# Input and block-boundary norms of a two-block network: from one token tile at a time to two

## The chip, the cores and the metric

The kernel runs on one core of one Trainium2 chip. The metric is the device time of one execution in microseconds (us); lower is better. Engines are named as in the profile: PE is TensorE, PEld its weight loads, DVE is VectorE, ACT is ScalarE, POOL is GpSimd, SP is SyncE (here it only issues DMAs). The result is one float32 tensor of 512 x 1024.

## The reference, cut to what matters

Two networks of two layers each run one after the other on 512 tokens of width 1024. The first begins with a layer norm of the input, and each of its layers ends in another; the second begins each half layer with an RMS norm that is scaled and shifted by a modulation vector:

```python
x = layer_norm(x, ln0_g, ln0_b)
for l in range(2):
    mix = hybrid_mixer(x, w_in[l], ...)
    x = layer_norm(alpha * x + mix, ln1_g[l], ln1_b[l])
    hid = square(relu(x @ w_up[l]))
    x = layer_norm(alpha * x + hid @ w_down[l], ln2_g[l], ln2_b[l])
for l in range(2):
    h = rms_norm(x, g_mix[l]) * (1.0 + sc_m) + sh_m
    z = h @ w_in_2[l] + b_in[l]
    ...
```

So the last layer norm of the first network (l = 1) is followed at once by the first RMS norm of the second. This place is called the boundary below; the norm of the input is called the start.

## The kernel before, in words

**Tiles.** The 512 tokens lie in four token tiles of 128 (tk = 0 to 3), 128 tokens on the partitions and 1024 features along the free axis. A matmul needs its activations the other way round, features on the partitions: `xTh` and `xTl`, the high and low part of a float32 number in two float32r tiles of 128 x 8 x 512. Every product is three matmuls (L235 to L237: high by high, then the two mixed ones). Weights come as 512 KB chunks (`wraw`, three buffers, issued on SP, L224), are rounded on ACT (`whi`, L228), and the rest is subtracted on DVE (`wlo`, L229).

**A norm of one tile.** `layer_norm` (L347) takes the statistics of two halves (`bn_stats`, L345), joins them (`bn_aggr`, L351), forms the reciprocal square root of the variance in `rsqrt` (L306) and applies both in one DVE instruction over the tile (L354). `rsqrt` has no table: it is an integer start value and three Newton steps on DVE. On a 128 x 1 operand that is nine instructions, three to start (L311, L316, L317) and three times two (L323, L324), each of which reads what the one before it wrote. On any other shape a step takes three (L326 to L328), twelve in all. `affine_T` (L356) then turns the tile: eight PE transposes (L336) in two halves into PSUM tiles `tr` (two buffers), eight ACT instructions that apply gain and offset column by column (`hT`, L364, operands `lnc` or `ge`, `mc`), and for each half a cast to `xTh` (DVE, L365) and a subtraction to `xTl` (L366; first half on DVE, second half on POOL). `lag` holds back `affine_T` in program order for one or two tiles.

**The start.** `first` (L1215) issues on SP the small table `cpack` (identity), the four tiles of `x`, the large table (L194), the two gain and offset columns `lnc` (L373), then the per-layer vectors and the first weight chunks. `norm_out` (L1016) takes the tiles one after another; the statistics of tiles 1 to 3 are ordered on DVE behind the norm of tile 0 (`issue_after`). The first product is the one for q: `lin_fm` with `early=2` (L256) makes two output tiles in two cuts of 256 tokens, so its first matmuls need token tiles 0 and 1, and its second cut tiles 2 and 3. `bias_setup` (L398) loads a one-hot table and the bias table on SP and prepares them with three DVE instructions (L407, L408, L411) for small matmuls that run much later (L416).

**The boundary.** The last product of the first network adds up in PSUM for the four token tiles in turn; `ffn1` (L963) adds each to `xo` (L989) and calls `after` (L1182). For the last layer that is, tile by tile: statistics, `bn_aggr` (L1190), subtract the mean and multiply by the gain row (L1192), `rsqrt`, multiply and add the offset row (L1195), a DMA out, the sum of squares on ACT (`Square` with an accumulator, L1199, into one of the two buffers `xhat`), and then `rms_tile` (L1307): a second `rsqrt`, a scaled copy on ACT into the same `xhat` (L1326), and `affine_T`. `rms_tile` of a tile is called one tile later than its layer norm, tiles 2 and 3 both at the end. Next in PE's order are the first gate tiles of the second network, again `early=2` in two cuts.

**What sets the order.** A planner orders the instructions of each engine when the program is built: of those whose inputs it believes ready it takes the earliest in program order. So the small instructions of one `rsqrt` are laid between the long ones of other tiles. On the chip each engine then runs its list in order.

Of the kernel before, what the change touches and what calls it, by code (L numbers as in the profile page):

```python
# [10 lines left out]
F32 = mybir.dt.float32  # L11
# [9 lines left out]
D = 1024  # L21
# [146 lines left out]
class Kern:  # L168
# [18 lines left out]
    def load_constants(self):  # L187
# [14 lines left out]
        nc.vector.memset(self.halfpi, math.pi / 2)  # L202

# [143 lines left out]
    def layer_norm(self, r, st):  # L347

        nc = self.nc
        mv = self.sm.tile([128, 2], F32, name="bnmv")  # L350
        nc.vector.bn_aggr(out=mv, in_=st)  # L351
        rs = self.sm.tile([128, 1], F32, name="rstd")
        self.rsqrt(rs, mv[:, 1:2], 1.0, self.e_ln)
        return nc.vector.tensor_scalar(r, r, mv[:, 0:1], rs, op0=OP.subtract, op1=OP.mult)  # L354
# [641 lines left out]
    def norm_tile(self, wk, pp, r, st, cols, tk, act, xd, lag):  # L996

        last = self.layer_norm(r, st)

        def turn():  # L1000
            self.affine_T(wk, pp, r, tk, cols[:, 0, :], cols[:, 1, :], act)
            self.nc.gpsimd.dma_start(xd[:, tk, :], r)

        self.lag(tk, turn, lag)
        return last
# [10 lines left out]
    def norm_out(self, wk, pp, r, cols, xd, act):  # L1016
        st = self.new_stats(wk)
        first = None
        for tk in range(4):
            with self.tc.issue_after(first.ins) if tk else ExitStack():  # L1020
                for half in range(2):
                    self.stats(st[:, tk], r[:, tk, :], half)
            done = self.norm_tile(wk, pp, r[:, tk, :], st[:, tk], cols, tk, act, xd, FILL["lag"][0])
            first = first or done

    def layer1(self, l, xd, act, start):
# [3 lines left out]
        with tc.tile_pool(name="mx", bufs=1) as mx:  # L1030
# [6 lines left out]
            with tc.tile_pool(name="at", bufs=2) as wk:  # L1037
# [31 lines left out]
                if l == 0:  # L1069
                    self.bias_setup(wk, pp)  # L1070
                    self.zero_images(wk)
# [102 lines left out]
        with tc.tile_pool(name="f1", bufs=1) as wk:  # L1174
# [6 lines left out]

            def after(tk, ch):  # L1182
# [5 lines left out]
                if last:  # L1188
                    mv = self.sm.tile([128, 2], F32, name="bnmv")
                    nc.vector.bn_aggr(out=mv, in_=st[:, tk])  # L1190
                    x = xo[:, tk, :]
                    nc.vector.scalar_tensor_tensor(out=x, in0=x, scalar=mv[:, 0:1], in1=g2, op0=OP.subtract, op1=OP.mult)  # L1192
                    rs = self.sm.tile([128, 1], F32, name="rstd")
                    self.rsqrt(rs, mv[:, 1:2], 1.0, self.e_ln)
                    nc.vector.scalar_tensor_tensor(out=x, in0=x, scalar=rs, in1=b2, op0=OP.mult, op1=OP.add)  # L1195
                    nc.gpsimd.dma_start(xd2[:, tk, :], x)
                    ss = self.sm.tile([128, 1], F32, name="rss")
                    xn = wk.tile([128, D], F32, name="xhat", bufs=2)
                    nc.scalar.activation(xn, x, AF.Square, accum_out=ss)  # L1199
                    box.append((x, ss, xn))  # L1200
                    for t in ((), (0,), (1,), (2, 3))[tk]:
                        xt, sst, xnt = box[1 + t]
                        self.rms_tile(wk, pp, xt, t, 0, 0, box[0], ss=sst, xn=xnt, lag=FILL["lag"][3])
# [11 lines left out]
    def first(self):  # L1215
# [6 lines left out]
        def start(wk):  # L1222
            xin = wk.tile([128, 4, D], F32, name="xin")
            for tk in range(4):
                nc.sync.dma_start(xin[:, tk, :], a["x"][tk * 128:(tk + 1) * 128, :])
            self.load_constants1()
            cols = self.ln_cols(wk, (0, 1))
# [79 lines left out]
    def rms_tile(self, wk, pp, x, tk, l, i, act, st=None, bufs=3, ss=None, xn=None, lag=0):  # L1307
# [3 lines left out]
        rs = self.sm.tile([128, 1], F32, name="rstd")  # L1311
        if ss is not None:
            self.rsqrt(rs, ss, 1.0 / D, self.e_rms)
        else:
# [494 lines left out]
```

## Time and profile before

| | us |
|---|---|
| median of 3 runs | 3738.05 (3736.97 to 3739.5) |
| the profiled execution | 3742.39 |
| its span, first instruction to last | 3740.6 |
| PE busy in the span | 3598.2 (96%) |
| DVE busy | 2237.3 (60%) |
| ACT busy | 1408.4 (38%) |
| POOL busy | 121.9 (3%) |

The profiled execution took 3742.39 us and its span covers 3740.6 of them; it lies 4.34 us above the median of the runs. Times in the rows further down are counted from the span's start. A busy share of PE holds waiting inside a pipelined matmul too, so where PE lost time is read from the stretches in which it had nothing to do, and from the clock it was granted there.

### The profile page before, as it was taken

To read this page: it belongs to the slowest core of one execution; us is meant where nothing else is said; L and a number is where in the kernel's file an instruction comes from. 1 tells how busy PE (TensorE), PEld (TensorE's weight loads), DVE (VectorE), ACT (ScalarE), POOL (GpSimd) and SP (SyncE) were. 2 spreads that over 40 slices of the span, in tenths; PEclk is the share of its full clock that TensorE was granted. 3 is DMA by queue.
4 is the path that set the end of the run, shared out by engine and by line. 5 is a ranking of instruction groups with operands and counts; after the bars stand their busy time and mean duration, and the time that the engine had idled before them with its cause. 6 is when DMAs were issued, how large, how long until landed. Compare 5 with 4: busy or idle time off the path is not lost. (4 is left out here: it accounts for less than half of the span.)

```text
span 3740.6 us, 54252 instructions
## 1 busy us (share of the span) xinstructions
PE 3598.2 (96%) x21232; PEld 2844.9 (76%) x21232; DVE 2237.3 (60%) x4799; ACT 1408.4 (38%) x2413; POOL 121.9 (3%) x209
## 2 busy tenths in 40 slices
PE   7999999899999999998999999999999999999999
PEld 6677776778877877766788777778888877778887
DVE  5667775765566577756745549765333479664333
ACT  4543333332334543332424234554222344633221
POOL 0000000000000000000000000000000000000000
PEclk9999999999999999999999999999999999999999
DMA  4333333555543333234655432334332323253322
GB/s 147 119 114 85 88 84 121 162 182 180 167 157 91 104 93 92 78 98 151 197 178 171 156 105 71 119 122 149 96 96 97 116 86 107 67 186 119 96 96 96
DMA packets 509520, 452.23 MB, mean 121 GB/s; under 512 B 88112, under 2 KB 405232, under 8 KB 509264
## 3 DMA queue, kind: packets, MB, share of 16 engines
q1 hardware_dynamic: 492032, 400.88, 35.1%
q0 software_dynamic: 10320, 32.15, 2.5%
q10 hardware_dynamic: 6912, 15.73, 1.2%
q8 instruction: 167, 2.74, 0.3%
q14 instruction: 89, 0.73, 0.1%
HBM read 395.68 MB, written 53.01 MB: 120 GB/s over the span
## 5 line engine op out<-in xcount | busy, mean ns | idle before, releaser
L229 DVE TENSOR_TENSOR wlo<-wraw,whi 128x1024 fp32r<-128x1024 f32 (+2 forms) x496 | 604.4, 1219 | 775.1 <-ACT whi L228 769.3
L228 ACT ACTIVATE whi<-wraw 128x1024 fp32r<-128x1024 f32 (+2 forms) x496 | 523.3, 1055 | 1419.8 <-PE tm L237 563.4
L235 PE MATMUL acc<-xTh,whi 128*128 128x512 f32 (+1 forms) x2320 | 913.0, 394 | 5.7 <-ACT whi L228 2.1
L237 PE MATMUL acc<-xTh,wlo 128*128 128x512 f32 (+1 forms) x2320 | 901.6, 389 | 3.5 <-DVE wlo L229 3.5
L236 PE MATMUL acc<-xTl,whi 128*128 128x512 f32 (+1 forms) x2320 | 897.1, 387 | 3.9 <-POOL xTl L366 1.9
L235 PEld LDWEIGHTS acc<-xTh,whi 128*128 128x128 f32 x2320 | 437.1, 189 | 106.8 <-issue 14.9
L237 PEld LDWEIGHTS acc<-xTh,wlo 128*128 128x128 f32 x2320 | 437.7, 189 | 93.0 <-DVE wlo L229 5.1
L236 PEld LDWEIGHTS acc<-xTl,whi 128*128 128x128 f32 x2320 | 438.1, 189 | 84.6 <-POOL xTl L366 4.0
L235 PE MATMUL tm<-whi,hidh 128*128 128x512 f32 x784 | 307.2, 392 | 1.3 <-DVE xo L989 1.2
L237 PE MATMUL tm<-whi,hidl 128*128 128x512 f32 x784 | 306.5, 391 | 0.0
L236 PE MATMUL tm<-wlo,hidh 128*128 128x512 f32 x784 | 306.5, 391 | 0.0
L236 PE MATMUL tm<-wlo,xTh 128*128 128x512 f32 (+1 forms) x448 | 169.7, 379 | 14.1 <-DVE wlo L229 14.1
L235 PEld LDWEIGHTS tm<-whi,hidh 128*128 128x128 f32 x784 | 147.2, 188 | 35.8 <-issue 2.0
L237 PEld LDWEIGHTS tm<-whi,hidl 128*128 128x128 f32 x784 | 147.2, 188 | 32.2
L236 PEld LDWEIGHTS tm<-wlo,hidh 128*128 128x128 f32 x784 | 147.2, 188 | 31.8
L237 PE MATMUL tm<-whi,xTl 128*128 128x512 f32 (+1 forms) x448 | 168.9, 377 | 0.0
L235 PE MATMUL tm<-whi,xTh 128*128 128x512 f32 (+1 forms) x448 | 167.7, 378 | 0.0
L1293 DVE SCALAR_TENSOR_TENSOR asum<-araw,cc,asum 128x768 f32<-128x768 f32 x112 | 113.8, 1016 | 43.5 <-DMA araw<-in_w_ada_dram 42.4
L1716 DVE TENSOR_TENSOR hT<-hT,acc 128x512 f32<-128x512 f32 x44 | 30.3, 688 | 132.5 <-PE acc L237 128.8
L236 PEld LDWEIGHTS tm<-wlo,xTh 128*128 128x128 f32 x448 | 85.4, 191 | 29.6 <-DVE wlo L229 15.0
L569 DVE CUSTOM_DVE_ANT_0 L<-lg,G 128x512 f32<-128x512 f32 (+3 forms) x128 | 73.5, 587 | 47.2 <-PE lg L1507 31.2
L570 ACT ACTIVATE L<-L,ast 128x384 f32<-128x384 f32 (+3 forms) x128 | 71.1, 556 | 69.8 <-DVE ast L569 68.9
(479 smaller groups left out, 5454.7 us busy)
## 6 DMA issues: line engine op xcount, KB each, us to landing
wraw<-in_w_in_dram SPq DMA_DIRECT2D x182, 512.0 KB, 3.9
wraw<-in_w_down_dram SPq DMA_DIRECT2D x108, 512.0 KB, 3.5
araw<-in_w_ada_dram SPq DMA_DIRECT2D x128, 384.0 KB, 3.9
wraw<-in_w_gu_dram SPq DMA_DIRECT2D x88, 512.0 KB, 3.8
wraw<-in_w_up_dram SPq DMA_DIRECT2D x64, 512.0 KB, 4.2
wraw<-in_w_out_dram SPq DMA_DIRECT2D x32, 512.0 KB, 3.6
wraw<-in_w_branch_dram SPq DMA_DIRECT2D x18, 512.0 KB, 3.5
prd<-gt POOLq DMA_DIRECT2D x32, 256.0 KB, 2.7
```

Of the source, the lines that this page charges most:

```text
L228: nc.scalar.activation(hi[:, :n], raw[:, :n], AF.Copy)
L229: nc.vector.tensor_tensor(out=lo[:, :n], in0=raw[:, :n], in1=hi[:, :n].bitcast(F32), op=OP.subtract)
L235: nc.tensor.matmul(ps, st[0], mv[0], start=start, stop=False)
L236: nc.tensor.matmul(ps, st[0], mv[1], start=False, stop=False)
L237: nc.tensor.matmul(ps, st[1], mv[0], start=False, stop=stop)
L569: nc.vector.tensor_tensor_reduce(L, ps, bias, -1.0, -LOW, OP.add, OP.min, nmx)
L570: nc.scalar.activation(L, L, AF.Exp, bias=nmx, scale=-1.0, accum_out=ssum)
L1293: nc.vector.scalar_tensor_tensor(out=acc, in0=w, scalar=cc[:, k:k + 1], in1=acc, op0=OP.mult, op1=OP.add)
L1716: nc.vector.tensor_tensor(out=t[j], in0=t[j], in1=ps, op=OP.mult)
```

## The change

The norm of the input and the layer norm and RMS norm at the boundary work on pairs of token tiles: one `rsqrt` of 128 x 2 for two tiles in place of two of 128 x 1. At the start the second pair's statistics are ordered behind the norm of tile 1. At the boundary the closing instructions of tiles 0 and 1 wait for the pair's root, and both RMS norms of a pair share a root, which is called behind the opening instructions of tile 2 for the first pair and at the end for the second. The one-tile chains of the other norms stay. Further: a first small ACT instruction in `load_constants`; the `lnc` loads move from behind the large table to behind the first tile of `x`; and `bias_setup`'s DVE instructions are ordered behind the norm of tile 3.

```diff
@@ -200,6 +200,8 @@
         self.fr = g("fr", 8)
         self.halfpi = self.cst.tile([128, 1], F32, name="halfpi")
         nc.vector.memset(self.halfpi, math.pi / 2)
+        warm = self.sm.tile([128, 1], F32, name="rstd")
+        nc.scalar.activation(warm, self.halfpi, AF.Identity)
 
     def dump(self, name, ap):
         if self.dumpf:
@@ -351,7 +353,7 @@
         nc.vector.bn_aggr(out=mv, in_=st)
         rs = self.sm.tile([128, 1], F32, name="rstd")
         self.rsqrt(rs, mv[:, 1:2], 1.0, self.e_ln)
-        return nc.vector.tensor_scalar(r, r, mv[:, 0:1], rs, op0=OP.subtract, op1=OP.mult)
+        nc.vector.tensor_scalar(r, r, mv[:, 0:1], rs, op0=OP.subtract, op1=OP.mult)
 
     def affine_T(self, wk, pp, x, tk, g, b, act, bufs=3):
 
@@ -995,14 +997,15 @@
 
     def norm_tile(self, wk, pp, r, st, cols, tk, act, xd, lag):
 
-        last = self.layer_norm(r, st)
-
+        self.layer_norm(r, st)
+        self.norm_end(wk, pp, r, cols, tk, act, xd, lag)
+
+    def norm_end(self, wk, pp, r, cols, tk, act, xd, lag):
         def turn():
             self.affine_T(wk, pp, r, tk, cols[:, 0, :], cols[:, 1, :], act)
             self.nc.gpsimd.dma_start(xd[:, tk, :], r)
 
         self.lag(tk, turn, lag)
-        return last
 
     def lag(self, tk, f, lag):
 
@@ -1014,14 +1017,25 @@
         return wk.tile([128, 4, 2, 6], F32, name="bnst", bufs=1)
 
     def norm_out(self, wk, pp, r, cols, xd, act):
+
         st = self.new_stats(wk)
-        first = None
-        for tk in range(4):
-            with self.tc.issue_after(first.ins) if tk else ExitStack():
-                for half in range(2):
-                    self.stats(st[:, tk], r[:, tk, :], half)
-            done = self.norm_tile(wk, pp, r[:, tk, :], st[:, tk], cols, tk, act, xd, FILL["lag"][0])
-            first = first or done
+        for t0 in (0, 2):
+            mv, rs = self.pair()
+            with self.tc.issue_after(self.normed.ins) if t0 else ExitStack():
+                for i in range(2):
+                    for half in range(2):
+                        self.stats(st[:, t0 + i], r[:, t0 + i, :], half)
+                    self.nc.vector.bn_aggr(out=mv[:, i, :], in_=st[:, t0 + i])
+                self.rsqrt(rs, mv[:, :, 1], 1.0, self.e_ln, tag="rp")
+            for i in range(2):
+                x = r[:, t0 + i, :]
+                self.normed = self.nc.vector.tensor_scalar(x, x, mv[:, i, 0:1], rs[:, i:i + 1],
+                                                           op0=OP.subtract, op1=OP.mult)
+                self.norm_end(wk, pp, x, cols, t0 + i, act, xd, FILL["lag"][0])
+
+    def pair(self):
+
+        return (self.sm.tile([128, 2, 2], F32, name="bnmv2", bufs=2), self.sm.tile([128, 2], F32, name="rstd2", bufs=2))
 
     def layer1(self, l, xd, act, start):
         nc, a, tc, pp = self.nc, self.a, self.tc, self.pp
@@ -1067,7 +1081,8 @@
                 self.lin_tm(pp, w_in, [(1536, 2048)], act, 8,
                             lambda t, ps: nc.scalar.activation(v[:, t, :], ps, AF.Copy))
                 if l == 0:
-                    self.bias_setup(wk, pp)
+                    with tc.issue_after(self.normed.ins):
+                        self.bias_setup(wk, pp)
                     self.zero_images(wk)
                 ya = yh("ya")
                 self.pool_branch(wk, pp, l, vec, act, ya)
@@ -1179,6 +1194,16 @@
             st = self.new_stats(wk)
             box = []
 
+            late = []
+
+            def rms(t0):
+                ss, xn = late.pop()
+                rs = self.sm.tile([128, 2], F32, name="rrs2", bufs=2)
+                self.rsqrt(rs, ss, 1.0 / D, self.e_rms, tag="rp")
+                for j in range(2):
+                    self.rms_tile(wk, pp, xo[:, t0 + j, :], t0 + j, 0, 0, box[0], rs=rs[:, j:j + 1], xn=xn[j],
+                                  lag=FILL["lag"][3])
+
             def after(tk, ch):
                 self.stats(st[:, tk], xo[:, tk, :], ch)
                 if ch == 0:
@@ -1186,21 +1211,29 @@
                 if not box:
                     box.append(self.xT())
                 if last:
-                    mv = self.sm.tile([128, 2], F32, name="bnmv")
-                    nc.vector.bn_aggr(out=mv, in_=st[:, tk])
-                    x = xo[:, tk, :]
-                    nc.vector.scalar_tensor_tensor(out=x, in0=x, scalar=mv[:, 0:1], in1=g2, op0=OP.subtract, op1=OP.mult)
-                    rs = self.sm.tile([128, 1], F32, name="rstd")
-                    self.rsqrt(rs, mv[:, 1:2], 1.0, self.e_ln)
-                    nc.vector.scalar_tensor_tensor(out=x, in0=x, scalar=rs, in1=b2, op0=OP.mult, op1=OP.add)
-                    nc.gpsimd.dma_start(xd2[:, tk, :], x)
-                    ss = self.sm.tile([128, 1], F32, name="rss")
-                    xn = wk.tile([128, D], F32, name="xhat", bufs=2)
-                    nc.scalar.activation(xn, x, AF.Square, accum_out=ss)
-                    box.append((x, ss, xn))
-                    for t in ((), (0,), (1,), (2, 3))[tk]:
-                        xt, sst, xnt = box[1 + t]
-                        self.rms_tile(wk, pp, xt, t, 0, 0, box[0], ss=sst, xn=xnt, lag=FILL["lag"][3])
+                    i, x = tk % 2, xo[:, tk, :]
+                    if i == 0:
+                        box.append(self.pair())
+                    mv, rs = box[-1]
+                    nc.vector.bn_aggr(out=mv[:, i, :], in_=st[:, tk])
+                    nc.vector.scalar_tensor_tensor(out=x, in0=x, scalar=mv[:, i, 0:1], in1=g2,
+                                                   op0=OP.subtract, op1=OP.mult)
+                    if i == 0:
+                        if tk:
+                            rms(0)
+                        return
+                    self.rsqrt(rs, mv[:, :, 1], 1.0, self.e_ln, tag="rp")
+                    ss = self.sm.tile([128, 2], F32, name="rss2", bufs=2)
+                    xn = [wk.tile([128, D], F32, name="xhat", bufs=2) for _ in range(2)]
+                    for j in range(2):
+                        x = xo[:, tk - 1 + j, :]
+                        nc.vector.scalar_tensor_tensor(out=x, in0=x, scalar=rs[:, j:j + 1], in1=b2,
+                                                       op0=OP.mult, op1=OP.add)
+                        nc.gpsimd.dma_start(xd2[:, tk - 1 + j, :], x)
+                        nc.scalar.activation(xn[j], x, AF.Square, accum_out=ss[:, j:j + 1])
+                    late.append((ss, xn))
+                    if tk == 3:
+                        rms(2)
                 else:
                     self.norm_tile(wk, pp, xo[:, tk, :], st[:, tk], cols, tk, box[0], xd2, FILL["lag"][2])
 
@@ -1223,8 +1256,9 @@
             xin = wk.tile([128, 4, D], F32, name="xin")
             for tk in range(4):
                 nc.sync.dma_start(xin[:, tk, :], a["x"][tk * 128:(tk + 1) * 128, :])
+                if tk == 0:
+                    cols = self.ln_cols(wk, (0, 1))
             self.load_constants1()
-            cols = self.ln_cols(wk, (0, 1))
             self.norm_out(wk, pp, xin, cols, xd, act)
             self.dump("x0", xd)
 
@@ -1304,14 +1338,12 @@
             nc.gpsimd.dma_start(md[g * 4:g * 4 + 4, :], row[::32, :])
             yield
 
-    def rms_tile(self, wk, pp, x, tk, l, i, act, st=None, bufs=3, ss=None, xn=None, lag=0):
+    def rms_tile(self, wk, pp, x, tk, l, i, act, st=None, bufs=3, rs=None, xn=None, lag=0):
 
         nc = self.nc
         k2 = self.k2[l]
-        rs = self.sm.tile([128, 1], F32, name="rstd")
-        if ss is not None:
-            self.rsqrt(rs, ss, 1.0 / D, self.e_rms)
-        else:
+        if rs is None:
+            rs = self.sm.tile([128, 1], F32, name="rstd")
             if st is None:
                 st = self.sm.tile([128, 2, 6], F32, name="bnst")
                 for j in range(2):
```

## Rows read from the trace of the kernel before

**Rows 1.** The page, busy time, share of the span and instructions of each engine

```profile
PE 3598.2 (96%) x21232; PEld 2844.9 (76%) x21232; DVE 2237.3 (60%) x4799; ACT 1408.4 (38%) x2413; POOL 121.9 (3%) x209
```

**Rows 2.** Four stretches: us, busy time (instructions) of each engine, granted clock (PEclk), DMA share, GB/s

```profile
2147.30:2160.70 13.40, 3.97 (x17) 3.14 (x16) 13.29 (x53) 9.35 (x19) 2.92 (x4) 0.64 0.19 78
2160.70:2177.20 16.50, 15.92 (x113) 15.18 (x114) 6.04 (x17) 11.28 (x26) 5.48 (x7) 0.88 0.20 47
9.40:21.40 12.00, 5.00 (x21) 3.85 (x21) 12.00 (x45) 8.98 (x19) 2.50 (x3) 1.00 0.86 248
21.40:38.50 17.10, 14.73 (x108) 14.28 (x108) 12.61 (x26) 8.06 (x20) 4.89 (x5) 1.00 0.45 147
```

**Rows 3.** Timeline of PE at the start: start, length, what, [idle before <-releaser]

```profile
21.39 0.58 PE L235 MATMUL acc<-xTh,whi 128*128 128x256 f32 x1 [0.64 <-DVE xTh L365]
...
28.76 0.63 PE L336 MATMUL tr<-cpack,xin 128*128 128x128 f32 x4 [2.19 <-DVE xin L354]
...
38.36 0.28 PE L237 MATMUL acc<-xTh,wlo 128*128 128x256 f32 x1
```

**Rows 4.** Timeline of DVE at the start

```profile
4.80 1.29 DVE L345 BATCH_NORM_STATS2 bnst<-xin 128x6 f32<-128x512 f32 x2 [3.91 <-DMA xin<-in_x_dram]
...
6.36 0.15 DVE L311 TENSOR_SCALAR rqv<-bnmv 128x1 f32<-128x1 f32 x1
...
8.61 0.81 DVE L354 TENSOR_SCALAR xin<-xin,bnmv,rstd 128x1024 f32<-128x1024 f32 x1
...
26.03 1.75 DVE L408 TENSOR_TENSOR t<-G,t 32x512 fp32r<-32x512 f32 x1
27.81 0.81 DVE L354 TENSOR_SCALAR xin<-xin,bnmv,rstd 128x1024 f32<-128x1024 f32 x1
```

**Rows 5.** Timeline of ACT at the start

```profile
10.79 1.28 ACT L364 ACT_TABLE_LOAD   x1 [10.79 <-DMA lnc<-in_lncol_dram]
...
29.49 2.93 ACT L364 ACTIVATE hT<-tr,lnc 128x128 f32<-128x128 f32 x8 [3.67 <-PE tr L336]
```

**Rows 6.** SP's timeline at the start, and the landing times of line 1225

```profile
3.65 0.95 SPq L373 DMA_DIRECT2D lnc<-in_lncol_dram  x2
...
DMA to landing us min/median/max: 3.6/4.9/6.2
```

**Rows 7.** Line 326, the first operation of a Newton step on wider operands: ns min/median/max

```profile
L326 DVE TENSOR_TENSOR rqt<-rqy x72: 123/164/193, 156.9 to 3117.2; 128x4 f32<-128x4 f32 x30, 128x8 f32<-128x8 f32 x24, 128x32 f32<-128x32 f32 x18
```

**Rows 8.** Timeline of DVE at the boundary

```profile
2138.98 0.68 DVE L989 TENSOR_TENSOR xo<-xo,tm 128x512 f32<-128x512 f32 x1
...
2141.92 1.28 DVE L1195 SCALAR_TENSOR_TENSOR xo<-xo,rstd,lnb 128x1024 f32<-128x1024 f32 x1
2143.12 0.15 DVE L311 TENSOR_SCALAR rqv<-bnmv 128x1 f32<-128x1 f32 x1
...
2144.56 0.15 DVE L311 TENSOR_SCALAR rqv<-rss 128x1 f32<-128x1 f32 x1
...
2149.65 0.21 DVE L324 TENSOR_SCALAR rstd<-rqt,rqy 128x1 f32<-128x1 f32 x1
```

**Rows 9.** Timeline of ACT at the boundary

```profile
2149.99 1.13 ACT L1326 ACTIVATE xhat<-xo,rstd 128x1024 f32<-128x1024 f32 x1
...
2155.09 1.09 ACT L1199 ACTIVATE xhat<-xo 128x1024 f32<-128x1024 f32 x1
...
2160.94 1.16 ACT L1326 ACTIVATE xhat<-xo,rstd 128x1024 f32<-128x1024 f32 x1
...
2168.23 2.91 ACT L364 ACTIVATE hT<-tr,mc,ge 128x128 f32<-128x128 f32 x8 [0.69 <-PE tr L336]
```

**Rows 10.** Timeline of PE at the boundary

```profile
2151.17 1.97 PE L336 MATMUL tr<-cpack,xhat 128*128 128x128 f32 x8 [3.84 <-ACT xhat L1326]
...
2160.72 0.80 PE L235 MATMUL tm<-xTh,whi 128*128 128x256 f32 x2 [1.39 <-DVE xTh L365]
...
2170.99 0.38 PE L236 MATMUL tm<-xTl,whi 128*128 128x256 f32 x1 [0.22 <-DVE xTl L366]
```

## The prediction

> **What bounds the kernel now.** I read the page first: PE is busy 96% of the span [rows 1], so a norm can matter only where PE has nothing to do. The table of stretches then shows the two places that the change touches [rows 2]. At the start PE is busy 5.00 of the 12.00 us before its first product, while DVE is busy for all 12.00, and 14.73 of the 17.10 us that the first two q tiles take. At the boundary PE is busy 3.97 of 13.40 us at a granted clock of 0.64, DVE 13.29, and then 15.92 of 16.50 us at 0.88. In both, DVE sets the pace: read its timeline, then see which ACT and PE rows hang on it. Beyond them PE is full, so a shift of the first product moves the end by as much.
>
> The profiled execution took 3742.39 us, 4.34 above the median of 3738.05. The sum below is a difference within that execution, and I lay it on the median. A measurement of this kernel tells about 0.2% from no change, 7.5 us.
>
> **The start: what is removed and added.** Now tile 0's statistics start at 4.80, its root at 6.36, its norm at 8.61 [rows 4]: 1.56 us for statistics and aggregate, 2.25 for the nine-step root, 0.81 for the norm. ACT can't use it: it waits for `lnc` until 10.79 and then loads its table for 1.28 [rows 5], so `hT` of tile 0 begins at 12.07.
>
> With pairs tile 0 waits for tile 1's data. The four tiles of x land 3.6 to 6.2 us after their issues [rows 6]; with four issues at the 0.48 that SP takes for one `lnc` issue, they arrive (2.6 + 1.4)/3 = 1.3 apart, so tile 1 at 6.1. The `lnc` issues now stand ahead of it: nothing at best, their whole 0.95 at worst; I take 0.5, in the middle, as the pieces are tiny but the queue is in order. From 6.6: statistics 1.56, root 2.3, norms at 10.5 and 11.3. The root's price isn't in the trace for this shape: twelve instructions at the 0.164 of a wider one [rows 7] are 2.0, at the 0.25 per instruction of the nine-step root 3.0; I take 0.19, nearer to the first, which has the same instruction.
>
> Tile 0's transposes then start at 11.3; half of their 1.97 [rows 10] later, at 12.4, `hT` begins, now with `lnc` long landed and the table loaded. So the pair costs tile 0 only 0.3 us, and tile 1 follows without a gap: 2.93 for tile 0 [rows 5] and half of that for tile 1 give 16.8, where before its own chain held it. The first matmul, at 21.39 [rows 3], can come at 17.5 if cast and subtraction follow at once, and at 20.1 if a weight rounding on ACT (as long as another 128 x 1024 instruction there, 1.13 [rows 9]) and a weight subtraction on DVE (1.75 at worst, by the one beside a busy POOL [rows 4]) both go first. I take 19.0: **2.4 us gained**.
>
> The second gain is a stall: PE waits 2.19 us at 28.76 for the norm of tile 3 [rows 3], which starts at 27.81 right behind the bias instruction of 1.75 [rows 4]. With bias behind it and the second pair's work (two times 1.56, root 2.3, two norms 1.6: 7.0 us from 12.0, with up to 4 of other work between, since this engine is full) that norm comes at 19 to 23. I take 1.8 of the 2.19 as gained; if the planner puts those transposes early among the matmuls, all of it may stay. Together **-4.2**, between -1.3 (20.1, stall kept) and -6.1 (17.5, stall gone).
>
> At nothing: the first ACT instruction, for ACT idles until 10.79; without that cover it would cost 1.28. If the table load stayed where it is, ACT would do it while waiting for the transposes. The bias instructions move into 17.10 us in which DVE is idle 4.5; uncovered they cost 1.75 and twice 0.81 at most, ahead of the next weight subtraction. Their SP loads keep their place; the large table and tiles 1 to 3 go 0.95 later on SP, the weights not. POOL's DMAs keep their number, and it is busy 2.92 of 13.40 us at its fullest place here.
>
> **The boundary.** Tile 1's sum starts at 2138.98 [rows 8]. Its opening takes 0.68, statistics of one half and aggregate 0.9 (1.56 less 0.65), and the mean and gain instruction 1.28, by its twin of that length: 2141.85. Then the pair's root 2.3, two closing instructions 2.4 (start to start 1.20), the Square of tile 1 with its read 1.3, the second root 2.3: 2150.15 if nothing comes between. But tiles 2 and 3 open in this stretch, 5.7 us on DVE, of which 1.3 fit under that Square. That gives 2154.55; I take T = 2154.2 for the first scaled copy, because the planner fills every gap of a chain with a longer instruction, as it does between 2144.56 and 2149.65, where one root takes 5.1 us [rows 8]. Before, that copy ran at 2149.99 [rows 9]; tile 0 loses 4.2 us, tile 1 much less, since its own chain is gone.
>
> From T: copy 1.13 and half the transposes, `hT` of tile 0 at T + 2.3; 2.9 for it and 1.3 for the Square of tile 2, which gets its `xhat` buffer when tile 0's transposes are done; half of tile 1's `hT` 1.5; cast 0.5. First matmul at T + 8.5 = 2162.7, against 2160.72 [rows 10]: +2.0. The second pair is held longer: both its Squares need `xhat` buffers, the last free after tile 1's transposes at T + 7.8, and both tiles wait for a shared root. Square 1.3, root 2.3 with 1.1 of casts between: copies at T + 12.5 = 2166.7, before at 2160.94 [rows 9]; two copies and transposes later `hT` of tile 3 starts at T + 17.5 = 2171.7, before 2168.23: +3.5, and with it the second cut, now at 2170.99 [rows 10]. Between +2.0 and +3.5 I take **+2.7**. At the bound without interposed work (T 4.05 earlier) it would be -2.0.
>
> Twenty-four DVE instructions disappear here (72 for 48). Do they cost their own length? The 1.28 us instruction at 2141.92 ends at 2143.20, and the next starts at 2143.12 [rows 8]: neighbours overlap, so a small one in a full list costs less than its length. The Trainium skill ("VectorE: DVE Perf Modes", section "The DRAIN you can't avoid") says that the next operation doesn't start until the pipe is empty, and to minimize the count; by that alone the 24 would return their 0.15 each, 3.6 us, and the boundary would come to -0.9. The row speaks against it.
>
> **Sum:** -4.2 + 2.7 = -1.5, 3736.5 us. By the bounds of its terms this case spans -4.1 to +2.2.
>
> **The rivals.** *The boundary comes out level*: T near the middle of its bounds (2152.2) puts the first matmul at 2160.7 and leaves only the start: 3733.9. For it: the engine list gets shorter. Against it: no gap in DVE's 13.29 of 13.40 us. *Both gain*: T at its lower bound (-2.0) and the start at its best (-6.1): 3729.9. For it stands the stall's clear cause; against it that all small costs must fall right.
>
> *Slower*: the second pair is held by the two `xhat` buffers. If tile 1's `hT` goes ahead of its Square whole (1.5 more) and its root is interlaced as before (5.1 for the 3.4 counted), PE is through its first cut and idle, and its clock falls again. The granted clock of 0.88 over 16.5 us means some 4 of them at 1.2 GHz in place of 2.4 and 2.0 lost; once more is 2.0. The boundary then costs 3.5 + 1.5 + 1.7 + 2.0 = 8.7, and beyond the 4.2 that the start gives this decides: 3742.5, or 3745.4 with the start at -1.3. For it: PE's clock of 0.64 there after waits. Against it: the first cut itself fills some 10 us of the wait (2160.72 to 2170.99 [rows 10]). The Trainium skill ("TensorE: Matmul & The Clock Gate", Part 1) says the same more sharply: the throttled clock is the default and activity releases it. The 0.64 agrees.
>
> **Chances.** The forecast 0.50, level 0.22, both gain 0.14, slower 0.14, of which 0.06 beyond 7.5 us. The first two and the milder part of the last lie within 0.2%: 0.80 the same, 0.14 faster, 0.06 slower. The range leaves out the ends: 3730 (both gain) to 3743.5 (a little above the milder slow case).
>
> **What would show it.** At the start: no table load behind 10.79, `hT` of tiles 0 and 1 back to back from about 12.4, first matmul near 19, no wait of 2 us before tile 3's transposes, the last row of the second cut near 34.4 in place of 38.36 [rows 3]. At the boundary: first scaled copy near 2154.2 less 4.2, both copies of a pair adjacent, first matmul 2 us later against tile 1's sum, the Squares of the second pair behind transposes. It is wrong if the copy comes less than 12 us after tile 1's sum (forecast 15.2), if the first matmul stays beyond 21, or if PE differs elsewhere by more than 2 us.

## The result, and the profile after the change

| | us |
|---|---|
| before, median of 4 runs | 3738.78 (3736.97 to 3739.92) |
| after, median of 4 runs | 3758.07 (3756.41 to 3759.93) |
| ratio | 1.0052, 95% interval 1.0037 to 1.0067 |
| the profiled execution after | 3757.78, span 3756.0 |

The change makes the kernel slower by 19.3 us; against the profiled execution of before the span is 15.4 us longer. The forecast was 3736.5, the range ended at 3743.5. Lines of the changed kernel from 203 on are numbered 2 higher, later ones more.

The page of the changed kernel, busy time and instructions of each engine, against [rows 1]:

```profile
PE 3613.2 (96%) x21232; PEld 2847.3 (76%) x21232; DVE 2232.2 (59%) x4763; ACT 1407.6 (37%) x2414; POOL 122.1 (3%) x209
```

This line already points to the answer. DVE did what the edit says: 36 instructions and 5.1 us less. PE has the same 21,232 matmuls and is busy 15.0 us longer. A wait in which PE stands empty would have left its busy time alone. So the loss is to be looked for in the matmuls themselves: in their pace, in the clock they are granted, or in waiting inside a pipelined matmul.

Four stretches of the changed kernel, in the columns of [rows 2]; the boundary's two are shifted, so that they meet at its first product as in [rows 2]:

```profile
2156.20:2169.60 13.40, 4.23 (x17) 3.03 (x17) 8.86 (x38) 9.39 (x21) 2.32 (x3) 0.50 0.29 117
2169.60:2186.10 16.50, 15.56 (x109) 14.44 (x110) 6.22 (x14) 10.07 (x22) 5.49 (x7) 0.90 0.08 15
9.40:21.40 12.00, 4.99 (x18) 3.50 (x18) 11.42 (x44) 7.57 (x18) 2.79 (x4) 1.00 1.02 310
21.40:38.50 17.10, 15.20 (x105) 14.97 (x106) 11.97 (x19) 8.00 (x20) 4.88 (x5) 1.00 0.39 124
```

At the boundary DVE is no longer full ahead of the first product (8.86 of 13.40 us, before 13.29): the list of DVE is shorter, and yet the product comes later. The start looks almost unchanged.

To find the rest, I set PE's rows of both traces side by side in their order and followed the difference of their times (after less before, both from the span's start):

```
us of the trace before     difference      what lies there
39                          +0.7           end of the start
200 to 1744                 -2.3           short waits, and stretches at a lower clock in the one or the other
1811 to 1817                +1.6           a stretch at a lower clock that the kernel before lacks: +4.0
1890 to 2130                +1.6 to +5.7   second product of a feed-forward (w_down): +4.1
2139 to 2161                +8.8           boundary: +3.1
2540 to 2940                +12.8          second network, first layer: merge, w_down: +4.0
2960 to 3310                +11.5
3330 to 3720                +15.4          second network, second layer: +3.9
```

Three times some 4 us accrue steadily, in stretches that the change doesn't touch (`w_down` is the weight of a feed-forward's second product, `merge` the product that joins the mixer's branches). The page's costliest groups show which matmuls they are, here of the changed kernel (busy, mean ns of one | idle before):

```profile
L237 PE MATMUL tm<-whi,hidh 128*128 128x512 f32 x784 | 310.9, 397 | 1.2 <-DVE xo L991 1.2
L239 PE MATMUL tm<-whi,hidl 128*128 128x512 f32 x784 | 310.3, 396 | 0.0
L238 PE MATMUL tm<-wlo,hidh 128*128 128x512 f32 x784 | 310.3, 396 | 0.0
```

and two of the same groups before, which the prediction had not looked at:

```profile
L235 PE MATMUL tm<-whi,hidh 128*128 128x512 f32 x784 | 307.2, 392 | 1.3 <-DVE xo L989 1.2
...
L237 PE MATMUL tm<-whi,hidl 128*128 128x512 f32 x784 | 306.5, 391 | 0.0
```

The same count and no waiting, and 5 ns more for each on the mean. PE's timeline tells it better, since a matmul's length overlaps its neighbours': what counts is start to start. After:

```profile
1899.74 0.39 PE L239 MATMUL tm<-whi,hidl 128*128 128x512 f32 x1
1899.97 0.40 PE L237 MATMUL tm<-whi,hidh 128*128 128x512 f32 x1
...
1901.61 0.39 PE L238 MATMUL tm<-wlo,hidh 128*128 128x512 f32 x1
1901.84 0.40 PE L239 MATMUL tm<-whi,hidl 128*128 128x512 f32 x1
```

Before:

```profile
1899.91 0.39 PE L237 MATMUL tm<-whi,hidl 128*128 128x512 f32 x1
...
1901.95 0.39 PE L237 MATMUL tm<-whi,hidl 128*128 128x512 f32 x1
```

Nine steps take 2.10 us after (233.3 ns each) and 2.04 before (226.7); the granted clock is 1.00 in both.

**The theory.** The change adds small tiles (two-tile means, roots and their scratch) to the pool `sm`, which grows from 2048 to 2368 bytes per partition. The pools of the weights (`wp`) and of `xTh`, `xTl` (`xp`) stand ahead of it, everything else behind: the activations move by 320 bytes, the weights don't. From the addresses that the tiles got in the built kernels, and the trace's spacing of consecutive products of 512 columns (`hid` is the hidden activation of a feed-forward, `ya` and `yb` the outputs of a mixer's branches, `mg` their merged sum; "later layers" are all but the first):

```
                                    address modulo 256 bytes    start to start,
product, where                      weights    activations      mean ns (pairs seen)
whi x hid, later layers, before       192        192             226.8 (1093)
whi x hid, later layers, after        192          0             233.3 (1093)
whi x mg, 2nd network, before         192        192             226.5 (128)
whi x mg, 2nd network, after          192          0             233.4 (128)
whi x hid, first layer, before        192        224             233.3 (457)
whi x ya, 1st network, before         192         96             233.4 (101)
whi x xTh, xTl, before and after      192        192             227.6 to 227.8 (over 3700)
```

In these groups products run at 227 ns where the two operands' addresses agree modulo 256 bytes and at 233 where they don't. Of 12,160 products of 512 columns, 1,912 have unlike operands before, 4,112 after: 2,200 x 6.5 ns = 14.3 us. That is somewhat high, for one group outside the table fits less well: `ya` and `yb` of the second network, alike before (192 and 192), differ by 64 bytes after (0 against 192) and run at 229 ns (some 350 pairs), 2 ns slower and not 6.5. **The rival**: the new chains themselves lose the time, by waits or by the clock.

### The profile page after: what moved, and what is told of

It reads as the page before. It is cut to its first block, busy times and chain, and to the rows that moved or that the text cites. A ratio compares the mean times of both kernels' runs of the same rounds, so it can differ in the third digit from the quotient of the medians.

```text
span 3756.0 us, 54218 instructions
## 1 busy us (share of the span) xinstructions
PE 3613.2 (96%) x21232; PEld 2847.3 (76%) x21232; DVE 2232.2 (59%) x4763; ACT 1407.6 (37%) x2414; POOL 122.1 (3%) x209
```

## The experiments

**1. The layout alone.** An unused tile in the kernel before, first in `sm` (the activations move, the weights don't), then in the pool `cst`, which stands ahead of both (all move together):

```diff
+        pad = self.sm.tile([128, 80], F32, name="pad", bufs=1)
+        nc.gpsimd.memset(pad[:, 0:1], 0.0)
```

> The kernel before, with nothing of the change, but with an unused tile of 320 bytes per partition in the pool of small tiles, so that every later tile lies exactly where the change puts it. Layout theory (a 512-column matmul takes 233 ns where the addresses of its two operands differ modulo 256 bytes, 227 where they agree; the change moved one of the two for some 1,850 matmuls): about 13 us slower than before, 3752, with the matmuls of the second down projection at 233 ns. Chain theory (the norms, and the clock that falls after their waits, cost all of it): as before, 3739.

> The kernel before with the same unused 320 bytes, but in the very first pool, so that both operands of every product move together: the hidden activations lie at the same absolute addresses as after the change, the weights move by 320 too. Layout theory by the difference of the operands: as before, 3739, matmuls at 227 ns. Layout theory by the absolute address of the hidden activations: as the changed kernel, about 3752. Chain theory: as before.

Measured (`before` in these larger sets stands some 4 us above the median of its 4 runs in the first table): in `sm` 3754.61 us against 3742.73, ratio 1.0033 (1.0020 to 1.0046); in `cst` 3741.34, ratio 0.9998 (0.9989 to 1.0007). PE's timeline of the first:

```profile
1899.65 0.40 PE L237 MATMUL tm<-whi,hidh 128*128 128x512 f32 x1
...
1901.05 0.40 PE L237 MATMUL tm<-whi,hidh 128*128 128x512 f32 x1
```

and of the second:

```profile
1899.74 0.39 PE L237 MATMUL tm<-whi,hidh 128*128 128x512 f32 x1
...
1901.10 0.39 PE L237 MATMUL tm<-whi,hidh 128*128 128x512 f32 x1
```

Six steps: 1.40 us (233 ns) against 1.36 (227). A tile that nobody uses costs 11.9 us (7.5 to 17.2), most of what the change costs; and it is the distance between the operands that counts, not the address of either.

**2. The change without the shift**, whole and each half alone. `sm` is created ahead of the two pools, so that weights and activations move together:

```diff
+        self.sm = P("sm", 4)
         self.wp = P("wp", 2)
         self.xp = P("xp", 1)
-        self.sm = P("sm", 4)
```

> The whole change, with the pool of small tiles created ahead of the weight and activation pools, so that its new size moves both operands of a product alike and their difference is again that of the kernel before. Layout theory: about 13 us come back, 3745, and what is left over the kernel before (about 6) belongs to start, boundary and clock. Chain theory: as the changed kernel, 3758.

> The start of the change alone (pairs at the input norm, early table load and columns, bias behind), boundary as before, operand differences as before. If the start costs what the two profiles show by the first cuts (0.7 us): 3739.5. My forecast for this part was -4.2: 3734.6. If the half-speed stretch that the changed kernel shows near 1811 us comes from the new phase that the start gives all later work, about 4 more: 3743.5.

> Only the boundary's pairs, with the start as it was and the small pool created ahead of the weights' pools, so that every pair of operands stands as before. Operand theory: within 3 us of the kernel before, with the wait at the boundary 2.5 to 3.5 us longer than before. Rival (the pairs at the boundary carry a loss of their own, xhat buffers and a lower granted clock): 6 us or more over it.

Measured: whole 3741.93 us, ratio 1.0000 (0.9991 to 1.0010); start alone 3742.22, 0.9997 (0.9988 to 1.0006); boundary alone 3745.63 against 3742.45, 1.0006 (0.9997 to 1.0015). PE of the whole change runs at 226.7 ns again. Without the shift the change can't be told from none; the 6 us that were expected to be left are not there. The traces resolve more than the medians: with the boundary alone, PE's rows fall back by 3.1 us between 2139 and 2161, as after (3.1). The rival of a large loss in the chains (6 us or more at the boundary) is out; a small one, 3.1 there and 0.6 at the start (below), lies inside the intervals.

**3. The change again**, beside the boundary alone of 2 and against the same runs of before, no edit:

> The changed kernel unaltered, on the same chip and against the same runs as its parts. Operand theory: 2,200 more of its 12,160 products of 512 columns have operands whose addresses differ modulo 256 bytes, at 6.5 us per thousand 14.3 us; with the rest of the change at nothing the time is 12 to 17 us over the kernel before. Rival (the start and the boundary cost time themselves, beside the layout): 17 to 21 us over it.

Measured: 3759.51 us against 3742.45, ratio 1.0044 (1.0029 to 1.0059), 17.1 us: at the border of the two expectations, and the interval (10.9 to 22.1) spans both. By rows this execution lost 1.4 at the start and 3.1 at the boundary (2139 to 2161, as above); with the 11.9 of the layout that is 16.4 of the 17.1. So the layout is most of it, and the rows speak for a small share of the rival; the medians alone decide neither.

**4. A shift that keeps the difference.** As in 1, with 256 bytes in place of 320:

```diff
+        pad = self.sm.tile([128, 64], F32, name="pad", bufs=1)
+        nc.gpsimd.memset(pad[:, 0:1], 0.0)
```

> The kernel before with an unused tile of 256 bytes in the small pool, where the tile of 320 bytes cost 12 us. Operand theory (what counts is the difference modulo 256 bytes): w_down's products of the last layers at 226.8 ns as before, time within 5 us of before (one look). Rival (any shift of the later tiles costs): 233.3 ns and 10 to 15 us more.

Measured: 3742.47 us in a single execution, the median of before beside it 3742.45. Its timeline:

```profile
1899.78 0.39 PE L238 MATMUL tm<-wlo,hidh 128*128 128x512 f32 x1
...
1901.14 0.39 PE L238 MATMUL tm<-wlo,hidh 128*128 128x512 f32 x1
```

Six steps in 1.36 us. A shift by 256 costs nothing, one by 320 costs 12 us. Other differences are in the table's groups: there 32, 64 and 96 bytes all cost the same, so the cost doesn't grow with the distance. The 229 ns of `ya` and `yb` at 64 bytes show that the size of the difference isn't the whole rule either; what else counts was not tried. A difference of 128 occurs only after (`whi` with `mg` in the first network, 192 against 64: 232.5 ns, before 233.4 at a difference of 64). And where the shift happens to make operands agree, they get faster: `y1`, another branch output, with `whi` 231.4 ns before (128 against 192) and 228.6 after, 32 pairs each.

**5. Before, with more of its operands alike.** If the theory holds, the kernel before has 1,912 products to mend. Unused tiles in the pools of four stages:

```diff
             with tc.tile_pool(name="at", bufs=2) as wk:
+                pad = wk.tile([128, 24], F32, name="pad", bufs=1)
...
             with tc.tile_pool(name="rw", bufs=1) as rw:
+                pad = rw.tile([128, 48], F32, name="pad", bufs=1)
...
         with tc.tile_pool(name="f1", bufs=1) as wk:
+            if not last:
+                pad = wk.tile([128, 56], F32, name="pad", bufs=1)
...
                 mg = (wk.tile([128, 8, S], F32R, name="mgh"), wk.tile([128, 8, S], F32R, name="mgl"))
+                pad = wk.tile([128, 16], F32, name="pad", bufs=1)
```

> The kernel before with four unused tiles of 96, 192, 224 and 64 bytes per partition that bring the addresses of ya, yb, mg, the first feed-forward's hid and some weight tails to agree with the weights' modulo 256 bytes: 432 products with unlike operands in place of 1,912. Operand theory: 1,480 x 6.5 ns = 9.6 us less than before (8 to 11), the first feed-forward's second product at 227 ns in place of 233. Rival (the 6.5 ns belong to something else that moved with the change, not to the difference of the addresses): within 2 us of before.

Measured: 3735.83 us against 3742.45, ratio 0.9983 (0.9974 to 0.9992): faster by 6.6, short of the 9.6, though the interval reaches 9.7. The first feed-forward's second product, before:

```profile
900.13 0.40 PE L235 MATMUL tm<-whi,hidh 128*128 128x512 f32 x1
...
900.83 0.40 PE L235 MATMUL tm<-whi,hidh 128*128 128x512 f32 x1
```

and with the four tiles:

```profile
900.44 0.39 PE L235 MATMUL tm<-whi,hidh 128*128 128x512 f32 x1
...
901.12 0.39 PE L235 MATMUL tm<-whi,hidh 128*128 128x512 f32 x1
```

Three steps in 0.70 and 0.68 us; over all 457 pairs the mean goes from 233.3 to 226.8, with `ya` from 233.4 to 228.4, with `mg` from 233.3 to 227.2. That product alone gains 4.7 us between 700 and 1070 us of the trace. Up to 700 us the `ya` and `yb` products, also faster, have moved nothing on balance (difference 0.1). PE stands idle for some 16 us between 500 and 700 us in both kernels, so that a gain can be lost in waits there; that it is lost so was not shown.

**6. Why the start gave nothing.** First, the loads of the norm's columns back behind the constants, in the start-alone kernel of 2:

```diff
                 nc.sync.dma_start(xin[:, tk, :], a["x"][tk * 128:(tk + 1) * 128, :])
-                if tk == 0:
-                    cols = self.ln_cols(wk, (0, 1))
             self.load_constants1()
+            cols = self.ln_cols(wk, (0, 1))
```

> The start alone (small pool ahead, boundary as before), with the loads of the norm's columns back behind the constants. The first product of 512 columns stands at 39.68 us before and at 40.26 with the change. Theory (the column loads ahead hold up x's second tile): the second tile's sums start at about 6.3 us instead of 7.65, the first transposes at about 11.2 instead of 12.46, and the first product of 512 columns at about 39.1. Rival (the second pair's root, held beside POOL's subtractions, sets the stage): the second tile is as early, but the first product of 512 columns stays within 0.3 us of 40.26.

Second, the other way round: the kernel before with the three orders and one tile at a time.

```diff
+        warm = self.sm.tile([128, 1], F32, name="rstd")
+        nc.scalar.activation(warm, self.halfpi, AF.Identity)
...
             first = first or done
+        self.normed = done
...
-                    self.bias_setup(wk, pp)
+                    with tc.issue_after(self.normed.ins):
+                        self.bias_setup(wk, pp)
...
+                if tk == 0:
+                    cols = self.ln_cols(wk, (0, 1))
             self.load_constants1()
-            cols = self.ln_cols(wk, (0, 1))
```

> The kernel before with the start's three orders alone (table load at the very start, columns' loads behind the first tile, bias operands behind the norms), and one tile at a time as before. Theory (the pairs lose what the orders gain): the table load of 1.28 us no longer stands ahead of tile 0's cut, first product at about 20.1 us instead of 21.39, first product of 512 columns at about 38.4 instead of 39.68. Rival (the orders themselves hold the stage): first product of 512 columns at 39.7 or later.

The first product of 512 columns ends the stage. Where it stands, and the first of 256 columns:

```
kernel                                           first of 256    first of 512
start as before, six executions                  21.37 to 21.78  39.65 to 40.05
the change's start, four executions              20.29 to 21.15  40.05 to 40.96
columns behind the constants                     19.06           38.28
the three orders, one tile at a time             21.41           38.20
```

The row of the first of these two runs, then of the second:

```profile
38.28 0.47 PE L237 MATMUL acc<-xTh,whi 128*128 128x512 f32 x1 [0.93 <-DVE q L1067]
```

```profile
38.20 0.47 PE L237 MATMUL acc<-xTh,whi 128*128 128x512 f32 x1 [0.92 <-DVE q L1056]
```

DVE of the changed kernel against DVE with the columns behind, up to the second tile's sums:

```profile
4.93 1.29 DVE L347 BATCH_NORM_STATS2 bnst<-xin 128x6 f32<-128x512 f32 x2 [4.04 <-DMA xin<-in_x_dram]
...
7.65 1.29 DVE L347 BATCH_NORM_STATS2 bnst<-xin 128x6 f32<-128x512 f32 x2 [1.20 <-DMA xin<-in_x_dram]
```

```profile
5.01 1.29 DVE L347 BATCH_NORM_STATS2 bnst<-xin 128x6 f32<-128x512 f32 x2 [4.13 <-DMA xin<-in_x_dram]
...
6.46 1.23 DVE L347 BATCH_NORM_STATS2 bnst<-xin 128x6 f32<-128x512 f32 x2
```

The two small loads ahead of tiles 1 to 3 make DVE wait 1.20 us for tile 1; with the loads behind there is no wait, and the stage ends at 38.28 in place of 40.26. PE's wait for tile 2 is shorter too: 0.94 and 0.41 us in place of 2.21. The forecast of that run (39.1) was too careful, its theory right. In the second run the first product doesn't come earlier (21.41, forecast 20.1), but the stage ends 1.5 us before that of the kernel before: the orders gain, though not where I had put it, and tile by tile the loads ahead don't hurt, because the second tile's sums wait for the first tile's norm anyway (they start at 9.41 us there). So it is the pair together with the loads ahead of it that loses 2 us. And the pair itself gains nothing that these runs show: with its best order it ends the stage at 38.28, one tile at a time with the three orders at 38.20. Times of these two runs: 3736.17 and 3743.74 us, before 3740.58, one execution each; they decide nothing.

**7. The version that beats both**: the start with the columns behind the constants, the boundary as before, `sm` ahead of the weights' pools, and the four tiles of 5 (one buffer of `rss` less, so that it fits):

```diff
-                    ss = self.sm.tile([128, 1], F32, name="rss")
+                    ss = self.sm.tile([128, 1], F32, name="rss", bufs=3)
```

> The start as in the run with the columns' loads back behind the constants, the boundary as before, the small pool ahead, and the four unused tiles of 96, 192, 224 and 64 bytes: 432 products of 512 columns with unlike operands in place of 1,912. Operand theory: 1,480 x 6.5 ns = 9.6 us, and 1.4 us from the start, 11 us less than before, 8 to 12.5. Rival (the start's gain is given back before the end, and the operands give what the run without it gave): 6 to 8 us less.

Measured: 3733.39 us against 3742.70, ratio 0.9973 (0.9964 to 0.9982): 0.27% faster than before. The 9.3 us lie within the forecast of 8 to 12.5; the interval, 6.7 to 13.5, doesn't shut out the rival's 6 to 8. The line of the second product that was slow in 1, now of this kernel:

```profile
L237 PE MATMUL tm<-whi,hidh 128*128 128x512 f32 x784 | 305.8, 390 | 1.2 <-ACT whi L230 1.1
```

390 ns on the mean, 392 before and 397 with the change.

## Why the prediction was wrong

**The step that failed** is "Beyond them PE is full, so a shift of the first product moves the end by as much". PE is full there, and I took a full PE for one whose pace the change can't touch. The sum priced the instructions that are added or moved, and no tile: the 320 bytes that the new tiles add to `sm`, and what stands behind them, are in no term of it. Experiment 1 puts 11.9 us on them, without any instruction of the change. The text did name the sign of it: "It is wrong [...] if PE differs elsewhere by more than 2 us"; it does, three times by 4.

**The start, forecast -4.2, measured +0.6** (39.68 to 40.26 for the first product of 512 columns), by its terms:

- The root of a pair: 0.19 for each of twelve instructions, right. They start some 0.2 apart from 9.22 to 11.39.
- Tile 1's data at 6.6: its sums started at 7.65. The column loads were given 0.5 us and cost more. This is why the transposes came at 12.46 (forecast 11.3), and 11.21 with the loads behind.
- The table load: at 0.75, hidden by ACT's idle time, right.
- `hT` of two tiles without a gap, right, but from 13.61 to 19.29 in place of 12.4 to 18.3 (12.4 and twice 2.93; the 16.8 of the sum is half of tile 1).
- First product at 19.0: 20.29, just beyond the bound of 20.1 (which its own terms, 17.5, 1.13 and 1.75, would put at 20.4); with the loads behind, 19.06.
- The stall of 2.19 us gone: it is there again, 2.21 long, in another place. ACT and PE of the changed kernel:

```profile
0.75 1.28 ACT L204 ACT_TABLE_LOAD   x1 [0.75 <-PEq L1829]
...
13.61 5.68 ACT L366 ACTIVATE hT<-tr,lnc 128x128 f32<-128x128 f32 x16 [11.37 <-PE tr L338]
```

```profile
20.29 0.58 PE L237 MATMUL acc<-xTh,whi 128*128 128x256 f32 x1 [2.62 <-DVE xTl L368]
20.68 0.41 PE L238 MATMUL acc<-xTl,whi 128*128 128x256 f32 x1
23.30 1.12 PE L338 MATMUL tr<-cpack,xin 128*128 128x128 f32 x4 [2.21 <-DVE xin L1032]
```

The norms came at 22.43, inside the forecast's 19 to 23, but the planner put tile 2's transposes third in PE's list. The prediction had this as its bound ("if the planner puts those transposes early among the matmuls, all of it may stay") and took the other end. With both bounds at the bad end its sum was -1.3; the delay of tile 1's data, which these bounds leave out, makes the difference up to +0.6 (with the loads behind, the stage ends 1.4 us earlier than before). The second pair's root was also held twice beside POOL:

```profile
17.08 1.26 POOL L368 TENSOR_TENSOR xTl<-hT,xTh 128x512 fp32r<-128x512 f32 x1 [3.10 <-DVE rpv L313]
21.12 1.26 POOL L368 TENSOR_TENSOR xTl<-hT,xTh 128x512 fp32r<-128x512 f32 x1 [2.78 <-DVE rpt L329]
```

```profile
17.14 1.23 DVE L318 TENSOR_SCALAR rpy<-rpv 128x2 int32<-128x2 int32 x1
...
21.14 1.25 DVE L330 SCALAR_TENSOR_TENSOR rstd<-rpt,rpy 128x2 f32<-128x2 f32 x1
```

Two values per partition take 1.23 us beside POOL's subtraction and 0.16 otherwise. The prediction knew this of a weight subtraction ([rows 4], "1.75 at worst, by the one beside a busy POOL") and didn't count it for the small instructions of the root.

**The boundary, forecast +2.7, measured +3.1** at its first product, is right, step by step. Against tile 1's sum (2144.74 after), the first scaled copy is at 14.7 us, forecast 15.2:

```profile
2144.74 0.69 DVE L991 TENSOR_TENSOR xo<-xo,tm 128x512 f32<-128x512 f32 x1 [1.22 <-PE tm L239]
...
2149.02 0.16 DVE L329 TENSOR_TENSOR rpt<-rpt,rpv 128x2 f32<-128x2 f32 x1
2149.10 0.68 DVE L991 TENSOR_TENSOR xo<-xo,tm 128x512 f32<-128x512 f32 x1
```

```profile
2159.48 1.15 ACT L1358 ACTIVATE xhat<-xo,rrs 128x1024 f32<-128x1024 f32 x1 [3.64 <-DVE rpt L328]
```

and the first product at 24.8 (forecast 23.7; 21.7 before), the second cut at 35.8 (35.5; 32.0 before, counted to the second cut's first product with `xTl`):

```profile
2169.57 0.80 PE L237 MATMUL tm<-xTh,whi 128*128 128x256 f32 x2 [2.62 <-DVE xTh L367]
...
2180.51 0.39 PE L238 MATMUL tm<-xTl,whi 128*128 128x256 f32 x1 [0.22 <-DVE xTl L368]
```

The second pair's copies come 27.9 us after the sum, forecast 27.7: shared root and `xhat` buffers as written.

```profile
2172.66 2.19 ACT L1358 ACTIVATE xhat<-xo,rrs 128x1024 f32<-128x1024 f32 x2 [2.39 <-DVE rrs L330]
```

The 24 instructions fewer did not pay visibly. At 2149.02 a small one and the next overlap by 0.08 us, as the prediction read it from [rows 8]. The prediction worked out -0.9 for the boundary from the sentence of the Trainium skill ("VectorE: DVE Perf Modes", section "The DRAIN you can't avoid") that the next operation waits for the empty pipe. That reading left out the section's own exception, that a next operation that is not held starts earlier; the overlap and the +3.1 agree with the exception.

**The rivals.** The slower one had the right sign and the wrong cause: no second fall of the clock (0.90 behind the first product, 0.88 before), and the second pair as forecast. The rivals were priced from waits, and from the lower clock after them; none was a change of PE's pace at the full clock.

**What stays open.** Of the 15.4 us between the two profiled executions 12.0 lie in the three slower stretches, 3.1 at the boundary, 0.6 at the start. The 4.0 near 1811 us and the 2.3 gained earlier belong to this execution and not to the change: the changed kernel's second execution (experiment 3) has neither (difference +2.9 at 1744 us, +3.0 at 1817). In the first one PE waits 3.38 us there for a `wlo` of DVE, and the granted clock is lower behind the wait,

```profile
1810.00:1815.00 5.00, 2.73 (x7) 2.15 (x7) 5.00 (x6) 0.56 (x1) 0.58 (x1) 0.59 0.20 53
```

as it is, behind 3.53 us, in the kernel before with the tile in `cst`, which is no slower:

```profile
1810.00:1815.00 5.00, 3.72 (x9) 2.95 (x10) 5.00 (x7) 0.00 (x0) 1.11 (x2) 0.50 0.41 112
```

In the kernel before and in the changed kernel's second execution PE waits 1.98 and 2.04 us there, and the clock stays at 1.00 (columns as in [rows 2]; the granted clock is third from the end). Why the wait is longer in one execution than in another was not tried. Nor was it settled whether the change without the shift costs the 3.9 us that its own rows show (0.8 at the start, 3.1 at the boundary by 2161 us; all but 0.7 are gone again by the end): its median shows no loss (ratio 1.0000), and its interval ends at 0.1%, 3.7 us.

## What to carry to other kernels

A change that adds a tile, however small, moves every pool behind it: before pricing its instructions, ask which operands of the busiest engine move against each other, and after it compare the start-to-start time of that engine's commonest instruction in stretches that the change doesn't touch. A busy time that grows at an equal count of instructions points at the pace of these instructions before it points at a wait for others; the start-to-start time tells. And a pair needs the data of both: whatever is put ahead of the second tile's load, however small, is paid by both tiles.

## What was not expected of the hardware

- In the large groups, products of 512 columns take 226.5 to 228 ns where both operands start at the same address modulo 256 bytes within a partition, and 231 to 235 where not: 3% on a matmul, 12 us on this kernel by one unused tile of 320 bytes. Not every group fits: the logits of the first network (k by q, equal addresses) stand at 231.8 ns in 85 pairs and the last weight chunks of the merged sum's product (`thi`, `tlo` with `mg`, first network, equal addresses) at some 231, while `ya` and `yb` of the second network after the change take 229 at a difference of 64. Why the chip does this no run here shows.
- A DVE instruction on two values per partition takes 1.23 us in place of 0.16 while POOL subtracts on 128 x 512. The Trainium skill ("GPSIMD Engine Reference", section "1. Specifications") has POOL's SBUF interfaces shared with VectorE, in contention with DVE instructions of two SBUF inputs or of a two-port mode. The trace agrees for L330, which has two inputs; L318, which has one, was held as well, and no row shows its mode.
- Two loads of tiny pieces ahead of a 512 KB tile made its data usable at least 1.2 us later (7.65 against 6.46), more than their 0.90 on SP. In three more executions with the loads ahead it was usable at 7.70 to 8.50, in one more with them behind at 6.68.
- At the start, products of 256 columns stand 0.21 us apart up to 24.3 us before and up to 29.1 after, and 0.12 from there on, while the granted clock of the stretch is 1.00 in both: that column alone doesn't show PE's pace there.
